# One residual, two engines: ScalarE scales four feature blocks of the mixer's reloaded residual, VectorE scales the other four inside its sums

## The chip, the cores and the metric

The kernel runs on one core of one Trainium2 chip. A core has five engines that take their own instruction streams in order and meet through semaphores: TensorE (PE; its weight loads are listed apart as PEld), VectorE (DVE), ScalarE (ACT), GpSimd (POOL) and SyncE (SP, here only an issuer of DMAs). The metric is the device time of one execution in microseconds; the kernel before takes 1076.38 us (median of three runs, 1075.28 to 1077.02).

## The reference

One decoder layer over 16 meta tokens and 512 real tokens with 1024 features: a SwiGLU feed-forward, a token mixer with two attention branches, a second feed-forward. All in float32. The change lies in the mixer's gates:

```python
def token_mixer(h, ...):
    proj = h @ w_in                       # h is rms_norm(residual, mix_norm)
    qa, ka, va, fa, qb, kb, vb, ga, gb = jnp.split(proj, idx, axis=-1)
    ...
    o_fox = fox_attention(qa, ka, va, log_f)
    o_swa = swa_attention(qb, kb, vb, swa_sinks, rel_bias_table)
    y = jax.nn.sigmoid(ga) * (o_fox @ w_branch_fox) + jax.nn.sigmoid(gb) * (o_swa @ w_branch_swa)
    return y @ w_out
```

`ga` and `gb` are products of the normalised residual with 2 x 1024 columns of `w_in`.

## The kernel before

**Number format.** A float32 product is made of three faster products. Each operand is split into a high part (ACT's cast, L133) and the rest (DVE's subtraction, L140); PE then does high x high (L301), high x rest (L302) and rest x high (L304). So every weight piece passes through ACT and then DVE before PE can use it: `raw` becomes `wh` and `wl`.

**Seven products for eight.** Two column blocks of weights (128 columns each) and the 512 tokens in two halves form a 2x2 block product, done with seven block products instead of eight (method `seven`). On the weights' side the pieces are A (a plain block, from `raw`), B (the sum `tc`, made by DVE from `rawC` and `rawD` in L233 and L234), C (`rawC`) and D (`rawD`, split into `wD`). On the activations' side the residual's features X (tokens in halves 0 and 1, features in halves 0 and 1) give A11, A12, A22 as they are and four sums: S3 = A11 - A21, S1 = A21 - A22, S2 = S1 - A11, S4 = A12 + S2. These are each a 128x1024 tile (four feature blocks of 128, each 256 tokens wide), and each is split like a weight (a cast and a subtraction). PE's order in one `seven` is A11 and S3 (with piece A), the S4 of the `seven` before, S2 and A22 (piece B), A12 and S1 (piece C). Each of the seven is 12 matmuls. After A11, ACT copies the accumulator `b` to a second bank `a` (L529), and PE then goes on adding S2 into `b`.

**The stage around the change.** After the attention, PE runs the last plain gate column, then six sliding-window branch products into `pt` banks, each copied out by ACT (L1722), and then the gates by `seven`: six of them in the order of the table `GATES`. To form the sums, the residual h1 is fetched again from DRAM by two DMAs on ACT's queue into `xg`, eight feature blocks of 128x512: blocks 0 to 3 by the first, 4 to 7 by the second. In the kernel before, ACT multiplies each of the eight blocks by the norm's gain `gmT` (L1728). S3 doesn't need `xg` (it is made of the split parts that still stand). DVE forms S1, S2 and S4 from `xg` (L1732, one instruction of 128x1024 each), into the tiles `at` that lie in `spare`. S4's sum is traced after the first `seven`.

**What sets the order.** No order is written out for the engines: a scheduler takes the traced program with its dependences and sets each engine's instruction order ahead of time; `after(...)` only puts the instructions of its block behind a named instruction on the same engine. On the chip each engine then follows its list. The other instructions that matter below are the gates' own arithmetic on DVE (L1754 before, L1766 after the change: products with `rb1`, `zA`, `oA`, `sg`), the sigmoids on ACT (L1794, then L1806) and the splits `yH`, `yL` of the finished gates. At the very start DVE scales the first token tiles by their norms (L649, L659), with the power on POOL (L351) in between; `gT` holds all gains and is fetched by SP's fourth DMA (L322), `gmT` is a slice of it.

Of the kernel before, what the change touches and what calls it, by code (L numbers as in the profile page):

```python
# [11 lines left out]
F32 = mybir.dt.float32  # L12
F32R = mybir.dt.float32r
AF = mybir.ActivationFunctionType
ALU = mybir.AluOpType
# [4 lines left out]
P = 128  # L20
D = 1024
KD = D // P
# [54 lines left out]
def run(steps):  # L77
    for f in steps:
        f()
# [3 lines left out]
def kernel(  # L83
# [22 lines left out]
    V, A, G, PE, SP = nc.vector, nc.scalar, nc.gpsimd, nc.tensor, nc.sync  # L106

    cp = ctx.enter_context(tc.tile_pool(name="const", bufs=1))
# [15 lines left out]
    def psum(whole=False):  # L124
        if banks["turn"] is not None:
            whole = banks["turn"] = not banks["turn"]
        tag = "pt" if whole else "ps"
        return pp.tile([P, 512], F32, tag=tag, name=nm(tag))

    def hi(o, i, scale=None):  # L130

        if scale is None:
            return A.copy(o, i)  # L133
        return A.activation(o, i, AF.Identity, scale=scale)

    def lo(o, i, h, scale=None):

        h = h.bitcast(F32)
        if scale is None:
            return V.tensor_tensor(out=o, in0=i, in1=h, op=ALU.subtract)  # L140
        else:
            return V.scalar_tensor_tensor(out=o, in0=i, scalar=scale, in1=h, op0=ALU.mult, op1=ALU.subtract)  # L142
# [59 lines left out]
    shared = {}  # L202
# [81 lines left out]
    def piece(ahead=None, then=None):  # L284

        c = state["use"]
        state["use"] += 1
        if then is not None and c in split:
            then(split[c])
            then = None  # L290
        split_to(c + (ahead or state["ahead"]))
        load_to(c + 5)
        if then is not None:
            then(split[c])
        return split.pop(c)
# [52 lines left out]
    gmT, g2T = gT[:, 1], gT[:, 2]  # L348
# [109 lines left out]
    class Units:  # L458
# [8 lines left out]
        def product(self, ps, name, w, half, more=False, first=True, last=True, src=None):  # L467

            h, l = (src or self.X.x)[name]
            n = len(h) if src else 4  # L470
            for k in range(n):
                prod(
                    [(ps[:, : self.th], h[k] if src else h[:, k], l[k] if src else l[:, k])],
                    w[0][:, n * half + k],
                    w[1][:, n * half + k],
                    k == 0 and first and not more,
                    k == n - 1 and last,
                    more,
                )
# [38 lines left out]
        def seven(self, use, last=False, src=None):  # L518

            th = self.th
            product = lambda *args: self.product(*args, src=src)
            b, a = psum(), psum(True)

            def p1(w):
                product(b, "A11", w, 0)
                A.copy(a[:, :th], b[:, :th])  # L529


            w = piece(None, p1)
            c = psum()
            product(c, "S3", w, 1)
            use("P7", c[:, :th])
            self.flush()
            w = piece()
            product(b, "S2", w, 0, True)
            d = psum(True)
            A.activation(d[:, :th], b[:, :th], AF.Identity, scale=-1.0)  # L540
            use("U2", b[:, :th])
            product(c, "A22", w, 1, True)
            use("C21 - U2", c[:, :th])
            w = piece()

            def p2():
                product(a, "A12", w, 1, True)
                use("C11", a[:, :th])

            def p5():  # L550
                product(d, "S1", w, 0, True)
                use("C22 + P7", d[:, :th])

            run([p5, p2] if last else [p2, p5])
            wd = piece(1 if last else None)

            def p3():
                product(d, "S4", wd, 0, True)
                use("C12", d[:, :th])

            self.pending = p3
            if last:
                self.flush()
# [44 lines left out]
    def after(*ins):  # L608

        st = ExitStack()  # L610
        for i in ins:
            st.enter_context(tc.issue_after(getattr(i, "ins", i)))
        return st
# [920 lines left out]
    for i in every:  # L1534
# [3 lines left out]
            out=zf[:n, i], in0=ps[:, 256:264], scalar=r1[:n, i : i + 1], in1=fb[:n], op0=ALU.mult, op1=ALU.add  # L1538
# [122 lines left out]
    halves = (slice(0, HF), slice(HF, S))  # L1661
# [17 lines left out]
    xg = gp.tile([P, KD, S], F32, tag="yH", name="xg")  # L1679
# [5 lines left out]
    at = [spare[:, 2 * i : 2 * i + 2].rearrange("p a (b c) -> p (a b) c", c=HF) for i in (0, 1, 2, 0)]  # L1685

    def parts_of(i, name):
        hi(xS[name][:, 0], at[i])
        lo(xS[name][:, 1], at[i], xS[name][:, 0])
# [34 lines left out]
    sliding(0, 1)  # L1724

    with after(*shared["split"]):
        for k in range(KD):
            A.activation(xg[:, k], xg[:, k], AF.Identity, scale=gmT[:, k : k + 1])  # L1728

    xq = lambda tok, feat: xg[:, 4 * feat : 4 * feat + 4, halves[tok]]  # L1730
    def sum_of(i, a, b, op=ALU.subtract):
        V.tensor_tensor(out=at[i], in0=a, in1=b, op=op)  # L1732

    parts_of(0, "S3")
    sum_of(1, xq(1, 0), xq(1, 1))
    sum_of(2, at[1], xq(0, 0))
    parts_of(2, "S2")
    parts_of(1, "S1")
    def last_sum():
        sum_of(3, xq(0, 1), at[2], ALU.add)  # L1740
        parts_of(3, "S4")

    sliding(*range(2, 6))

# [4 lines left out]
    class Gates:  # L1749
        th = HF  # L1750
# [73 lines left out]
    for i, step in enumerate(GATES):  # L1824
        if step[0] == "sliding":
            run(branch_steps(1, step[1], (oW, oLs), last_y(step[1])))
            gg.flush()
            continue
        b, m = step
        gg.seven(gate(m, b), False, src)  # L1830
        if i == 0:
            last_sum()
# [190 lines left out]
```

## Time and profile before

| what | value |
|---|---|
| median of three runs | 1076.38 us (1075.28 to 1077.02) |
| profiled execution | 1075.56 us, of it span 1073.5 us |
| granted TensorE clock | 0.999 of full speed |
| busy: PE, PEld | 1063.2 us (99%), 1031.0 us |
| busy: DVE, ACT, POOL | 892.0 us (83%), 654.6 us (61%), 211.7 us (20%) |
| ACT's scaling of `xg` (L1728) | 8 instructions, median 717 ns, from 604.4 to 610.2 us |
| DVE's sums from `xg` (L1732) | 3 instructions of 1217 to 1224 ns |

How to read it: times in the trace count from the first instruction of the span. A row of the timeline gives start, busy time, engine, line, operation, the tiles written and read, their shape, the count of merged instructions, and in brackets how long the engine had been idle before it and what ended that. Neighbouring instructions overlap in their pipelines, so the distance from start to start, not the busy time, is what one costs its engine. For PE the starts of neighbouring matmuls are the thing to look at.

### The profile page before, as it was taken

To read this page: it belongs to the slowest core of one execution; us is meant where nothing else is said; L and a number is where in the kernel's file an instruction comes from. 1 tells how busy PE (TensorE), PEld (TensorE's weight loads), DVE (VectorE), ACT (ScalarE), POOL (GpSimd) and SP (SyncE) were. 2 spreads that over 40 slices of the span, in tenths; PEclk is the share of its full clock that TensorE was granted. 3 is DMA by queue.
4 is the path that set the end of the run, shared out by engine and by line. 5 is a ranking of instruction groups with operands and counts; after the bars stand their busy time and mean duration, and the time that the engine had idled before them with its cause. 6 is when DMAs were issued, how large, how long until landed. Compare 5 with 4: busy or idle time off the path is not lost.

```text
span 1073.5 us, 22262 instructions
## 1 busy us (share of the span) xinstructions
PE 1063.2 (99%) x8515; PEld 1031.0 (96%) x8515; DVE 892.0 (83%) x1725; ACT 654.6 (61%) x1235; POOL 211.7 (20%) x281
## 2 busy tenths in 40 slices
PE   9999999999999999999999999999999999999998
PEld 8999999999999999999878799999999999999998
DVE  7988878888889678789897799888989788877895
ACT  7667456656666455556667766555665466745664
POOL 3011111121124442232200110001122111221120
PEclk9999999999999999999999999999999999999999
DMA  8787777688776314212211874567689777887763
GB/s 279 203 217 164 187 193 198 151 216 219 175 182 178 123 61 126 75 60 73 89 60 42 241 183 125 184 207 195 170 198 194 179 190 170 187 192 196 158 125 101
DMA packets 112570, 173.57 MB, mean 162 GB/s; under 512 B 10880, under 2 KB 59264, under 8 KB 112208
## 3 DMA queue, kind: packets, MB, share of 16 engines
q1 hardware_dynamic: 74464, 122.72, 36.2%
q0 software_dynamic: 29040, 37.83, 22.6%
q10 hardware_dynamic: 8960, 11.60, 3.4%
q8 instruction: 66, 1.08, 0.4%
q14 instruction: 40, 0.33, 0.1%
HBM read 167.89 MB, written 6.32 MB: 162 GB/s over the span
## 4 chain that ended last, share of the span: by engine, by line
PE 47%; DVE 5%; ACT 2%; DMA 1%; issue 1%; POOL 0%; ACTq 0%; SPq 0%; DVEq 0%; POOLq 0%
PE ps L301 8%; PE ps L304 8%; PE ps L302 8%; PE pt L301 7%; PE pt L302 7%; PE pt L304 7%; DVE wl L140 1%; DMA raw<-in_wg_dram 1%; ACT t L1209 1%; ACT wh L133 1%; DVE pL L140 1%; PE ps L1473 0%; PE ps L1938 0%; DVE S L140 0%; PE pt L1473 0%
## 5 line engine op out<-in xcount | busy, mean ns | idle before, releaser
L301 PE MATMUL ps<-x,wh 128*128 128x256 f32 (+2 forms) x768 | 219.7, 286 | 0.1
L302 PE MATMUL ps<-x,wh 128*128 128x256 f32 (+2 forms) x768 | 218.9, 285 | 0.5 <-DVE x L142 0.4
L304 PE MATMUL ps<-x,wl 128*128 128x256 f32 (+2 forms) x768 | 218.9, 285 | 0.0
L140 DVE TENSOR_TENSOR wl<-raw,wh 128x1024 fp32r<-128x1024 f32 (+3 forms) x125 | 150.1, 1201 | 39.8 <-ACT wh L133 38.9
L133 ACT CAST wh<-raw 128x1024 fp32r<-128x1024 f32 (+3 forms) x125 | 128.4, 1029 | 87.7 <-PE ps L302 52.5
L301 PEld LDWEIGHTS ps<-x,wh 128*128 128x128 f32 x768 | 144.7, 189 | 1.7 <-ACT hT L686 0.3
L302 PEld LDWEIGHTS ps<-x,wh 128*128 128x128 f32 x768 | 144.5, 188 | 1.4 <-DVE x L142 0.9
L304 PEld LDWEIGHTS ps<-x,wl 128*128 128x128 f32 x768 | 144.6, 188 | 0.9
L301 PE MATMUL pt<-x,wh 128*128 128x256 f32 (+2 forms) x424 | 125.3, 296 | 0.5 <-ACT wh L133 0.5
L304 PE MATMUL pt<-x,wl 128*128 128x256 f32 (+2 forms) x424 | 124.6, 294 | 0.0
L302 PE MATMUL pt<-x,wh 128*128 128x256 f32 (+2 forms) x392 | 112.5, 287 | 0.0
L133 ACT CAST wh<-tc 128x1024 fp32r<-128x1024 f32 (+1 forms) x70 | 71.8, 1026 | 65.1 <-DVE tc L234 55.7
L140 DVE TENSOR_TENSOR wl<-tc,wh 128x1024 fp32r<-128x1024 f32 (+1 forms) x70 | 83.5, 1192 | 32.4 <-ACT wh L133 32.0
L301 PE MATMUL ps<-acts,wh 128*128 128x264 f32 (+1 forms) x352 | 100.5, 285 | 0.1
L304 PE MATMUL ps<-acts,wl 128*128 128x264 f32 (+1 forms) x352 | 99.8, 284 | 0.0
L302 PE MATMUL ps<-acts,wh 128*128 128x264 f32 (+1 forms) x352 | 99.6, 283 | 0.0
L140 DVE TENSOR_TENSOR wl<-rawC,wh 128x1024 fp32r<-128x1024 f32 (+1 forms) x70 | 84.1, 1201 | 5.9 <-ACT wh L133 5.5
L133 ACT CAST wh<-rawC 128x1024 fp32r<-128x1024 f32 (+1 forms) x70 | 71.6, 1023 | 22.7 <-PE pt L302 17.7
L301 PEld LDWEIGHTS pt<-x,wh 128*128 128x128 f32 x424 | 79.9, 189 | 2.8 <-ACT wh L133 0.7
L304 PEld LDWEIGHTS pt<-x,wl 128*128 128x128 f32 x424 | 79.7, 188 | 2.1
L302 PEld LDWEIGHTS pt<-x,wh 128*128 128x128 f32 x392 | 73.8, 188 | 0.6
L301 PEld LDWEIGHTS ps<-acts,wh 128*128 128x128 f32 x352 | 66.5, 189 | 0.7 <-DVE h2T L918 0.3
(445 smaller groups left out, 3238.8 us busy)
## 6 DMA issues: line engine op xcount, KB each, us to landing
rawC<-in_w1i_dram SPq DMA_DIRECT2D x20, 512.0 KB, 5.1
raw<-in_w1i_dram SPq DMA_DIRECT2D x40, 256.0 KB, 4.5
raw<-in_w2i_dram SPq DMA_DIRECT2D x40, 256.0 KB, 3.3
rawC<-in_w2i_dram SPq DMA_DIRECT2D x20, 512.0 KB, 4.3
raw<-in_wm_dram SPq DMA_DIRECT2D x18, 512.0 KB, 4.3
raw<-in_wout_dram SPq DMA_DIRECT2D x16, 512.0 KB, 4.3
rawD<-in_w1i_dram SPq DMA_DIRECT2D x20, 256.0 KB, 4.3
raw<-in_w1i_dram POOLq DMA_DIRECT2D x20, 256.0 KB, 4.9
```

What stands on the lines that cost most here:

```text
L133: return A.copy(o, i)
L140: return V.tensor_tensor(out=o, in0=i, in1=h, op=ALU.subtract)
L301: PE.matmul(ps, sH, mH, start=first, stop=False, **more)
L302: PE.matmul(ps, sH, mL, start=False, stop=False, **more)
L304: shared["mm"] = PE.matmul(ps, sL, mH, start=False, stop=last, **more)
L1209: shared["exp"] = A.activation(t, t, AF.Exp, bias=nmx, scale=-1.0, accum_out=l[:, j : j + 1])
```

## The change

ACT now scales only blocks 0 to 3. A new small tile `less` holds minus the gains of blocks 4 to 7. DVE forms S1 and S4 with four SCALAR_TENSOR_TENSOR instructions each (block times gain, plus the other operand), one per feature block of 128x256; S2 stays one TENSOR_TENSOR. S4's two splitting instructions are put behind the first `seven`'s copy of `b` (L529).

```diff
             def p1(w):
                 product(b, "A11", w, 0)
-                A.copy(a[:, :th], b[:, :th])
+                shared["copy"] = A.copy(a[:, :th], b[:, :th])
...
     with after(*shared["split"]):
-        for k in range(KD):
+        for k in range(4):
             A.activation(xg[:, k], xg[:, k], AF.Identity, scale=gmT[:, k : k + 1])
+    less = cp.tile([P, 4], F32, name="less")
+    V.tensor_scalar(less, gmT[:, 4:KD], -1.0, None, op0=ALU.mult)
 
     xq = lambda tok, feat: xg[:, 4 * feat : 4 * feat + 4, halves[tok]]
-    def sum_of(i, a, b, op=ALU.subtract):
-        V.tensor_tensor(out=at[i], in0=a, in1=b, op=op)
+
+    def add_scaled(i, tok, by, to):
+        for k in range(4):
+            V.scalar_tensor_tensor(
+                out=at[i][:, k],
+                in0=xg[:, 4 + k, halves[tok]],
+                scalar=by[:, k : k + 1],
+                in1=to[:, k],
+                op0=ALU.mult,
+                op1=ALU.add,
+            )
 
     parts_of(0, "S3")
-    sum_of(1, xq(1, 0), xq(1, 1))
-    sum_of(2, at[1], xq(0, 0))
+    add_scaled(1, 1, less, xq(1, 0))
+    V.tensor_tensor(out=at[2], in0=at[1], in1=xq(0, 0), op=ALU.subtract)
     parts_of(2, "S2")
     parts_of(1, "S1")
     def last_sum():
-        sum_of(3, xq(0, 1), at[2], ALU.add)
-        parts_of(3, "S4")
+        add_scaled(3, 0, gmT[:, 4:KD], at[2])
+        with after(shared["copy"]):
+            parts_of(3, "S4")
```

The scheduler's lists differ in three places that matter. In the rows below a tile's name is followed by running numbers; `spare` holds the sums.

DVE at the head of the gates, before (`zA` is the last plain gate's product, L1709):

```order
L1709 TENSOR_TENSOR zA_4879<-zA_4879,spare_8183 128x512
L1732 TENSOR_TENSOR spare_8183<-xg_8197 128x1024
L140 TENSOR_TENSOR S3_1355_8196<-spare_8183,S3_1355_8196 128x1024
L1732 TENSOR_TENSOR spare_8183<-spare_8183,xg_8197 128x1024
L140 TENSOR_TENSOR S1_1347_8184<-spare_8183,S1_1347_8184 128x1024
L140 TENSOR_TENSOR wl_1369_8305<-raw_1360_8211,wh_1368_8304 128x1024
L140 TENSOR_TENSOR S2_1356_8198<-spare_8183,S2_1356_8198 128x1024
L233 TENSOR_TENSOR tc_1372_8336<-rawC_1364_8255,rawD_1365_8256 128x512
L140 TENSOR_TENSOR wD_1384_8411<-rawD_1365_8256,wD_1384_8411 128x512
L234 TENSOR_TENSOR tc_1372_8336<-tc_1372_8336,rawC_1364_8255 128x512
L1732 TENSOR_TENSOR spare_8183<-xg_8197,spare_8183 128x1024
L140 TENSOR_TENSOR wl_1374_8340<-tc_1372_8336,wh_1373_8339 128x1024
```

The same place after the change:

```order
L1736 SCALAR_TENSOR_TENSOR spare_8183<-xg_8197,less_8292 128x256
L1709 TENSOR_TENSOR zA_4879<-zA_4879,spare_8183 128x512
L1736 SCALAR_TENSOR_TENSOR spare_8183<-xg_8197,less_8292 128x256 x3
L1747 TENSOR_TENSOR spare_8183<-spare_8183,xg_8197 128x1024
L140 TENSOR_TENSOR S3_1355_8196<-spare_8183,S3_1355_8196 128x1024
L140 TENSOR_TENSOR S1_1347_8184<-spare_8183,S1_1347_8184 128x1024
L140 TENSOR_TENSOR S2_1356_8198<-spare_8183,S2_1356_8198 128x1024
L140 TENSOR_TENSOR wl_1369_8306<-raw_1360_8211,wh_1368_8305 128x1024
L233 TENSOR_TENSOR tc_1372_8337<-rawC_1364_8255,rawD_1365_8256 128x512
L140 TENSOR_TENSOR wD_1384_8412<-rawD_1365_8256,wD_1384_8412 128x512
L234 TENSOR_TENSOR tc_1372_8337<-tc_1372_8337,rawC_1364_8255 128x512
L1736 SCALAR_TENSOR_TENSOR spare_8183<-xg_8197,gT_82,spare_8183 128x256 x4
```

One of S1's four instructions now stands ahead of L1709, the rest right behind it; the splits of S3, S1, S2 and of the first weight piece follow in a block, then the sum `tc` of the first `seven`. Behind S4's four instructions come the splits of `tc` and `rawC`, and then S4's, which before stood behind six more rows. At the very start of DVE's list, the row `less` (L1730) has been placed between the first L649 and the first L659.

PE where S2 of the first `seven` begins, before and then after (`ps_1377` is bank b, `pt_1378` bank a, `wh_1373` and `wl_1374` are piece B, `wh_1379` is piece C):

```order
L304 MATMUL ps_1382_8396<-S3_1355_8196,wl_1369_8305 128x256
L301 MATMUL ps_1377_8373<-S2_1356_8198,wh_1373_8339 128x256
L302 MATMUL ps_1377_8373<-S2_1356_8198,wh_1373_8339 128x256
L301 MATMUL pt_1378_8374<-x_620_4306,wh_1379_8388 128x256
L304 MATMUL ps_1377_8373<-S2_1356_8198,wl_1374_8340 128x256
```

```order
L304 MATMUL ps_1382_8397<-S3_1355_8196,wl_1369_8306 128x256
L301 MATMUL ps_1377_8374<-S2_1356_8198,wh_1373_8340 128x256
L302 MATMUL ps_1377_8374<-S2_1356_8198,wh_1373_8340 128x256
L304 MATMUL ps_1377_8374<-S2_1356_8198,wl_1374_8341 128x256
L301 MATMUL ps_1377_8374<-S2_1356_8198,wh_1373_8340 128x256
```

The first matmul with piece C, which stood third in S2's run before, now stands behind S2's and A22's 24 matmuls.

ACT in the sixth and last `seven`, before and then after (`wh_1493` is its piece B, `wh_1497` its piece C, L529 its copy of b):

```order
L133 CAST yH_8371<-oA_4878 128x256 x2
L133 CAST wh_1493_9086<-tc_1492_9083 128x1024
L1794 ACTIVATE sg_1485_9036<-u2_1484_9032 128x256
L1794 ACTIVATE sg_1489_9058<-gz_1488_9056 128x256
L133 CAST wh_1497_9105<-rawC_1481_9001 128x1024
L529 COPY pt_1496_9091<-ps_1495_9090 128x256
```

```order
L133 CAST yH_8372<-oA_4878 128x256 x2
L1806 ACTIVATE sg_1485_9040<-u2_1484_9036 128x256
L1806 ACTIVATE sg_1489_9062<-gz_1488_9060 128x256
L133 CAST yH_8372<-oA_4878 128x256
L529 COPY pt_1496_9095<-ps_1495_9094 128x256
L1806 ACTIVATE sg_1491_9083<-c22_1490_9080 128x256
L133 CAST yH_8372<-oA_4878 128x256
L133 CAST wh_1493_9090<-tc_1492_9087 128x1024
L133 CAST wh_1497_9109<-rawC_1481_9005 128x1024
```

The casts of pieces B and C of the last `seven` now stand behind the copy of its bank b. DVE's list moved with it (`tc`'s second half L234 stands twelve rows behind the row that reads `u2` from its bank, where it stood one row behind it; most of what has come between is gate arithmetic), and on PE two matmuls with `wh_1497` and two of A22 stand ahead of the first matmul with piece B's rest.

## Prediction

> **What bounds the kernel now.** I read the page first (who is busy), then the windows around the change (who is idle there), then PE's timeline in the one window that isn't full, and last the timelines of the engines that feed it.
>
> ```profile
> PE 1063.2 (99%) x8515; PEld 1031.0 (96%) x8515; DVE 892.0 (83%) x1725; ACT 654.6 (61%) x1235; POOL 211.7 (20%) x281
> ```
>
> PE is the bound, so an edit on ACT and DVE is worth only what it changes in PE's gaps. By stretches (busy us of PE, PEld, DVE, ACT, POOL; clock; DMA share; GB/s):
>
> ```profile
> 604.00:611.00 7.00, 7.00 (x32) 5.67 (x31) 1.78 (x3) 6.61 (x12) 1.73 (x2) 1.00 1.06 344
> 611.00:618.00 7.00, 7.00 (x32) 5.66 (x31) 7.00 (x7) 5.64 (x8) 1.72 (x2) 1.00 0.76 140
> 618.00:628.00 10.00, 9.40 (x77) 8.99 (x76) 9.92 (x14) 7.39 (x13) 0.86 (x1) 1.00 0.68 195
> 628.00:638.00 10.00, 10.00 (x87) 10.00 (x86) 9.51 (x17) 6.27 (x13) 2.45 (x3) 1.00 0.74 189
> ```
>
> PE is full except from 618 to 628, where 0.60 us is missing. DVE idles 5.22 us from 604 to 611 and is nearly full from then on. DVE's late start is what the change can reach, and that one gap is where it can pay. PE's rows at the gap, where S2 of the first seven begins:
>
> ```profile
> 620.52 0.28 PE L302 MATMUL ps<-S,wh 128*128 128x256 f32 x1
> 620.64 0.28 PE L304 MATMUL ps<-S,wl 128*128 128x256 f32 x1
> 621.04 0.38 PE L301 MATMUL ps<-S,wh 128*128 128x256 f32 x1
> 621.27 0.28 PE L302 MATMUL ps<-S,wh 128*128 128x256 f32 x1
> 622.02 0.39 PE L301 MATMUL pt<-x,wh 128*128 128x256 f32 x1 [0.47 <-ACT wh L133]
> 622.25 0.28 PE L304 MATMUL ps<-S,wl 128*128 128x256 f32 x1
> ```
>
> Undisturbed starts lie 0.12 us apart (620.52 to 620.64; 0.118 over longer runs). From 620.64 to 622.25 are four steps, 0.47 us; they take 1.61. So **1.14 us** is lost, partly before the first row (bank b's copy) and mostly before the piece C matmul, which waits for ACT's cast of `rawC`.
>
> Why these are late, first ACT, then DVE:
>
> ```profile
> 606.62 1.34 ACT L1728 ACTIVATE xg<-xg,gT 128x512 f32<-128x512 f32 x2
> ...
> 608.33 2.57 ACT L1728 ACTIVATE xg<-xg,gT 128x512 f32<-128x512 f32 x4
> ...
> 618.18 0.59 ACT L1722 COPY oA<-pt 128x512 f32<-128x512 f32 x1 [1.54 <-PE pt L304]
> 619.67 1.06 ACT L133 CAST wh<-tc 128x1024 fp32r<-128x1024 f32 x1 [0.89 <-DVE tc L234]
> 620.63 0.36 ACT L529 COPY pt<-ps 128x256 f32<-128x256 f32 x1
> 620.93 1.04 ACT L133 CAST wh<-rawC 128x1024 fp32r<-128x1024 f32 x1
> ```
>
> ```profile
> 606.28 0.69 DVE L1709 TENSOR_TENSOR zA<-zA,spare 128x512 f32<-128x512 f32 x1 [1.27 <-ACT spare L1708]
> 610.93 1.22 DVE L1732 TENSOR_TENSOR spare<-xg 128x1024 f32<-128x1024 f32 x1 [3.95 <-ACT xg L1728]
> 612.07 1.22 DVE L140 TENSOR_TENSOR S<-spare,S 128x1024 fp32r<-128x1024 f32 x1
> ...
> 617.75 0.68 DVE L233 TENSOR_TENSOR tc<-rawC,rawD 128x512 f32<-128x512 f32 x1
> 618.35 0.68 DVE L140 TENSOR_TENSOR wD<-rawD,wD 128x512 fp32r<-128x512 f32 x1
> 618.95 0.68 DVE L234 TENSOR_TENSOR tc<-tc,rawC 128x512 f32<-128x512 f32 x1
> 619.55 1.22 DVE L1732 TENSOR_TENSOR spare<-xg,spare 128x1024 f32<-128x1024 f32 x1
> 620.76 1.23 DVE L140 TENSOR_TENSOR wl<-tc,wh 128x1024 fp32r<-128x1024 f32 x1
> ```
>
> The last four scalings hold ACT from 608.33 to 610.9. DVE waits for them (3.95 us), starts at 610.93, and reaches `tc` with L234 only at 618.95; ACT waits for that, and the copy of b and the cast of `rawC` queue behind its cast of `tc`.
>
> **The change part by part.**
>
> *Removed: four scalings on ACT*, 2.57 us to the end of the last, 0.62 us each. ACT isn't the bound there.
>
> *DVE's start.* It then waits for the second half of `xg` itself:
>
> ```profile
> L1732 DVEq EVENT_SEMAPHORE  x2: 21/36/50, 607.6 to 607.7; - x2
> DMA to landing us min/median/max: 8.4/9.8/11.2
> ```
>
> DVE's queue saw its waits end at 607.6 to 607.7 (the first row is of L1732, the second of `xg`'s two DMAs). The slower landing, 11.2 us, fits the second DMA. So the sums start at 607.7 instead of 610.93, 3.2 us earlier, with ACT's first four blocks ready (606.62 + 1.34, just before 608.0; the first of S1's four needs only the first of them). L1709 waits behind the first of the four and moves from 606.28 to about 608.1; its product is read only by the second branch's gates, which come behind the first two sevens.
>
> *Added: eight SCALAR_TENSOR_TENSOR for two TENSOR_TENSOR.* The trace has the same form (three SBUF float32 operands, 128x256, a gain per partition), and a two-operand row of that size beside it:
>
> ```profile
> 736.69 1.67 DVE L1863 SCALAR_TENSOR_TENSOR x<-h2T,gT,rb 128x256 f32<-128x256 f32 x4
> 682.25 1.42 DVE L140 TENSOR_TENSOR yL<-oA,yH 128x256 fp32r<-128x256 f32 x4
> ```
>
> With a last instruction of 0.48 and 0.41 us, steps are p = 0.40 and 0.34 us. A group of four is 1.6 us against 1.14 (610.93 to 612.07) for one wide instruction: 0.9 us more on DVE for both groups. The Trainium skill's Vector Engine (DVE) Microarchitecture Reference, section 7, Points that are easy to get wrong, says that this form with two SBUF sources that aren't bf16 halves the throughput. The two rows don't bear that out (a factor 1.18); what it would do is the third rival.
>
> *DVE's new timetable.* Up to `wl<-tc` it does S1's group (4p), L1709 (0.60, the step of the 128x512 rows), the sum for S2 and four splits (5 x 1.14 = 5.70), L233, `wD`, L234 (3 x 0.60), S4's group (4p), and the split of `tc` (1.23): 607.7 + 9.33 + 8p = 617.0 + 8p, **620.2** at p = 0.40. L234 starts at 607.7 + 1.6 + 0.6 + 5.7 + 1.2 = 616.8, before 618.95. ACT's cast of `tc` starts 0.72 after that, as now: 617.5 to 618.5; `rawC`'s follows to 619.5; the last `oA` copy to 620.0; L529 to 620.4. PE wants bank b at 620.76 (0.12 after 620.64) and `wl<-tc` at 621.0. Margins: 0.4 and 0.8 us. The piece C matmul now comes 24 matmuls later, at 623.6. So the gap closes: **-1.14 us**. Its bounds: -0.60, if only what the window shows as idle comes back, and -1.14, because PE's neighbouring stretches are full and can't give more. I take -1.14, since starts are what PE's pace shows.
>
> *S4's split behind L529*: ACT casts it at about 620.4, DVE subtracts it by 622.5; PE uses S4 after the second seven's S3, six products of 12 x 0.118 behind 620.76, at 629.2. Nothing waits.
>
> *`less`*: one small instruction in DVE's list at the start, where it waits for `gT`:
>
> ```profile
> 2.11 0.43 SPq L322 DMA_DIRECT2D gT<-in_gains_dram  x1
> DMA to landing us min/median/max: 4.9/4.9/4.9
> 6.91 0.75 DVE L659 TENSOR_SCALAR xt<-xt,rin 128x1024 f32<-128x1024 f32 x1 [0.83 <-POOL rin L351]
> 8.07 0.15 DVE L649 TENSOR_SCALAR rin<-rin 128x1 f32<-128x1 f32 x1 [0.41 <-ACT sq L634]
> ```
>
> `gT` lands at 2.1 + 4.9 = 7.0, DVE would have gone on at 6.91; with 0.15 for the instruction L659 slips about 0.25 us. Behind it DVE idles 0.41 before the next L649, which hides it: 0. If `gT` came later than about 7.2, the excess would lie on the path; bounds 0 and +0.3.
>
> *The last seven.* DVE and ACT run there in PE's rhythm, so I shift these rows by -1.14 and re-add them in the new order:
>
> ```profile
> 665.81 0.41 DVE L1754 TENSOR_TENSOR u<-ps,u 128x256 f32<-128x256 f32 x1
> 666.14 0.68 DVE L234 TENSOR_TENSOR tc<-tc,rawC 128x512 f32<-128x512 f32 x1
> 666.91 1.05 ACT L133 CAST wh<-tc 128x1024 fp32r<-128x1024 f32 x1 [0.58 <-DVE tc L234]
> 671.60 0.28 PE L301 MATMUL ps<-S,wh 128*128 128x256 f32 x1
> ```
>
> The `u` row now stands ahead of L233 and of one `oA` product: 665.81 - 1.14 - 0.60 - 0.34 = 663.73. Up to L234 follow L233 (0.60) and eleven steps of 0.335, `u` among them: 668.0. ACT's cast of `tc` 0.77 later, 668.8, ends 669.8; that of `rawC` (0.95 behind) ends 670.8. DVE's split of `tc` comes after L234 and four products, 668.0 + 0.60 + 1.34 = 670.0, and ends 671.2. PE starts S2 at 671.60 - 1.14 = 670.46 and wants `rawC`'s cast at the third matmul, 670.70, and `wl<-tc` at the seventh, 671.17. Both are level with their supply: **+0.2**, bounds 0 (DVE runs ahead) and +1.2 (one more DVE split or ACT round trip late).
>
> *Sum*: -1.14 + 0 + 0.2 = -0.9 us. The profiled execution, 1075.56, would be 1074.6; the median of the runs is 0.8 above it, so **1075.4 us**.
>
> **The rivals.**
>
> *The head start doesn't come.* DVE now depends on the second `xg` landing alone. The DMA share is 1.06 from 604 to 611, the busiest stretch here; 0.8 us later (608.5) uses up the margin, 2 us later gives the old gap back. Against: 607.7 was seen. Time: 1076.4.
>
> *The last seven takes it back* (the slower side). PE's list is fixed, and its third S2 matmul there stands behind two ACT casts, which stand behind twelve DVE rows with sigmoid round trips between them. Each us late is a us on PE. Above 1.14 the kernel is slower; a chain 2 us late gives 1076.4 - 1.14 + 2 = 1077.3. For: no margin, by the sum above. Against: most of what was put ahead is ready when DVE comes to it.
>
> *The dear form.* If a step of four is double the plain 0.335, p = 0.67, the split of `tc` ends at 622.4, 1.4 late at PE: 0.3 worse than the gap now, with the last seven 1076.9. It decides from p = 0.50 (level) and 0.64 (gain gone).
>
> **How the numbers follow.** Forecast (gap closed, up to 0.5 lost): 62 in 100. No head start: 13. Last seven: 15, about a third of it by more than 2 us net. Dear form: 3. Something unseen, either way: 7. A measurement here tells about 0.2% (2.15 us) from no change. The largest gain that PE's gap allows is half of that, so faster needs something unseen: 0.07. Slower needs a net 2.15: 0.08. Same: 0.85. The range takes the forecast with the runs' scatter (their median lies 0.6 and 1.1 from their ends) and the first two rivals: 1074.2 to 1077.2.
>
> **What would show it.** In the profile after: four L1736 rows on DVE from about 607.7, 1.6 us long; ACT's cast of `tc` at about 617.5; PE's starts 0.12 apart through S2 of the first seven, and PE full from 618 to 628; L659 at about 7.2 with the first L649 behind it unmoved; in the last seven, PE's third S2 matmul with a wait of 0.2 or less. The prediction is wrong if the gap stays, if a new one opens from 668 to 672, or if PE's starts stretch anywhere else by a microsecond.

## The result and the profile after

| | kernel before | change |
|---|---|---|
| median | 1076.01 us (1074.75 to 1078.31, 22 runs) | 1074.68 us (1073.81 to 1075.95, 22 runs) |
| span of the profiled execution | 1073.5 us | 1071.9 us |
| busy PE, DVE, ACT | 1063.2, 892.0, 654.6 us | 1062.0, 893.3, 652.8 us |

The ratio of the times is 0.9987, with a 95% interval of 0.9981 to 0.9993: 1.3 us less, between 0.75 and 2.0. The size is close to the sum that the prediction worked out (-0.9 us). Where it comes from is another matter: the runs below put about 0.7 us of it behind the gates, and some 0.15 us ahead of them, on something the prediction doesn't contain, and leave the rest of the gain, in the mixer's gates, at a size that depends on when a DMA lands.

First what the profile after shows of the predicted steps. The windows around the change (busy us of PE, PEld, DVE, ACT, POOL; clock; DMA share; GB/s):

```profile
604.00:611.00 7.00, 7.00 (x32) 5.68 (x31) 5.11 (x8) 6.35 (x10) 1.99 (x3) 1.00 1.01 323
618.00:628.00 10.00, 10.00 (x86) 9.92 (x85) 9.51 (x15) 7.25 (x13) 1.72 (x2) 1.00 0.74 197
```

DVE works 5.11 us from 604 to 611 where it worked 1.78, and the 0.60 us that PE lacked from 618 to 628 are there. DVE's timeline, from the second landing of `xg` on, and the landings of `xg`'s two DMAs:

```profile
606.60 0.49 DVE L1736 SCALAR_TENSOR_TENSOR spare<-xg,less 128x256 f32<-128x256 f32 x1 [1.85 <-DMA xg<-h1d]
607.01 0.69 DVE L1709 TENSOR_TENSOR zA<-zA,spare 128x512 f32<-128x512 f32 x1
607.61 1.27 DVE L1736 SCALAR_TENSOR_TENSOR spare<-xg,less 128x256 f32<-128x256 f32 x3
...
616.41 1.67 DVE L1736 SCALAR_TENSOR_TENSOR spare<-xg,gT,spare 128x256 f32<-128x256 f32 x4
617.99 1.22 DVE L140 TENSOR_TENSOR wl<-tc,wh 128x1024 fp32r<-128x1024 f32 x1
```

```profile
DMA to landing us min/median/max: 7.6/8.9/10.3
```

A group of four takes 1.58 us from start to start (616.41 to 617.99): the forecast's 1.6. The landing came after 10.3 us and not 11.2, so DVE began at 606.60 and not at 607.7; from there its list ran as worked out (split of `tc` finished 12.6 us later, 12.5 forecast). ACT and PE at the start of S2:

```profile
619.35 0.36 ACT L529 COPY pt<-ps 128x256 f32<-128x256 f32 x1
619.62 1.05 ACT L133 CAST S<-spare 128x1024 fp32r<-128x1024 f32 x1
620.60 1.05 ACT L133 CAST wh<-raw 128x1024 fp32r<-128x1024 f32 x1
621.55 0.37 ACT L1817 COPY p<-ps 128x256 f32<-128x256 f32 x1
```

```profile
620.52 0.28 PE L301 MATMUL ps<-S,wh 128*128 128x256 f32 x1
620.64 0.27 PE L302 MATMUL ps<-S,wh 128*128 128x256 f32 x1
...
621.82 0.28 PE L304 MATMUL ps<-S,wl 128*128 128x256 f32 x1
621.97 0.39 PE L301 MATMUL ps<-x,wh 128*128 128x256 f32 x1
622.20 0.28 PE L302 MATMUL ps<-x,wh 128*128 128x256 f32 x1
```

The copy of b is done long before PE wants the bank, and S2 runs in steps of 0.12. But A22's first matmul has steps of 0.15 and 0.23 about it, 0.14 us lost: its bank is emptied by the copy L1817, which now stands behind two casts, S4's among them. That wait is new.

The prologue, and the last seven (PE, then ACT):

```profile
7.04 0.17 DVE L1730 TENSOR_SCALAR less<-gT 128x4 f32<-128x4 f32 x1 [0.86 <-DMA gT<-in_gains_dram]
7.12 0.75 DVE L659 TENSOR_SCALAR xt<-xt,rin 128x1024 f32<-128x1024 f32 x1
8.09 0.15 DVE L649 TENSOR_SCALAR rin<-rin 128x1 f32<-128x1 f32 x1 [0.23 <-ACT sq L634]
```

```profile
670.46 0.28 PE L301 MATMUL ps<-S,wh 128*128 128x256 f32 x1
670.59 0.28 PE L302 MATMUL ps<-S,wh 128*128 128x256 f32 x1
670.83 0.39 PE L301 MATMUL pt<-x,wh 128*128 128x256 f32 x1
...
671.43 0.28 PE L304 MATMUL ps<-S,wl 128*128 128x256 f32 x1
```

```profile
669.73 1.05 ACT L133 CAST wh<-rawC 128x1024 fp32r<-128x1024 f32 x1
```

`less` holds L659 back by 0.21 and the next L649 by 0.02: hidden. In the last seven S2 begins at 670.46 as forecast, the third matmul waits for the cast of `rawC` that ends at 670.8, and the first product with piece B's rest starts at 671.43, 0.26 behind an undisturbed 671.17; 0.23 of this is lost about the third matmul.

Now the whole timetable of PE, before against after. PE's first 128x256 matmul of the gates starts at 617.93 before and 617.69 after; the first matmul of the last seven's last product at 675.86 and 674.96. So the gates are 57.93 and 57.27 us long: **0.66 us** gained, of 0.94 forecast. Beside the losses at A22 (0.14) and in the last seven (0.26), some 0.2 us are lost at 659 us, where PE passes to a product with `wD` (under 0.1 before); no row names the cause. 0.24 had come earlier (two executions of the kernel before differ by 0.36 there, from PE's first matmuls on; experiment 8 comes back to the 0.24). That makes 0.90 at 675 us; yet near the end of the span the lead is 1.57. The remaining 0.7 us arise in the second feed-forward, whose instructions the change doesn't touch. Two landmarks there, the second L368 row behind the gates (it spreads the second normalisation's factors for one half of the tokens) and the first transposition of the output, before and then after (the line numbers of the latter differ with the source):

```profile
735.59 0.61 PE L368 MATMUL ps<-ident,r 128*128 128x128 f32 x4
1046.12 1.18 PE L1938 MATMUL ps<-ident,h2T 128*128 128x128 f32 x8
```

```profile
734.73 0.61 PE L368 MATMUL ps<-ident,r 128*128 128x128 f32 x4
1044.56 1.20 PE L1950 MATMUL ps<-ident,h2T 128*128 128x128 f32 x8
```

310.53 us before, **309.83 us** after, with PE busy throughout in both, no wait that differs by more than 0.1 us, and a granted clock of 1.00 over the stretch in every execution shown here. Call this the second stretch; it gets experiments of its own.

### The profile page after: what moved, and what is told of

The parts are those of the page before. It is cut to its first block, busy times and chain, and to the rows that moved or that the text cites. A ratio compares the mean times of both kernels' runs of the same rounds, so it can differ in the third digit from the quotient of the medians.

```text
span 1071.9 us, 22258 instructions
## 1 busy us (share of the span) xinstructions
PE 1062.0 (99%) x8515; PEld 1029.7 (96%) x8515; DVE 893.3 (83%) x1732; ACT 652.8 (61%) x1231; POOL 211.8 (20%) x281
## 4 chain that ended last, share of the span: by engine, by line
PE 50%; DVE 3%; ACT 2%; issue 0%; DMA 0%; POOL 0%; ACTq 0%; DVEq 0%; POOLq 0%
PE ps L301 8%; PE ps L304 8%; PE ps L302 8%; PE pt L301 7%; PE pt L302 7%; PE pt L304 7%; ACT t L1209 1%; DVE wl L140 1%; ACT wh L133 1%; DVE pL L140 1%; PE ps L1473 0%; PE ps L1950 0%; PE pt L1473 0%; DMA raw<-in_wbr_dram 0%; DVE t L1212 0%
```

## The experiments

In all, PE's *gates* are the stretch from the first 128x256 matmul of the first seven to the last product of the last seven (57.93 us before), and the *second stretch* lies between the two landmarks above (310.53 us before).

**1. Both kernels once more.** The unchanged kernels, to see what differs from execution to execution.

> The changed kernel once more, unaltered. In its first profile PE's rows ran 0.24 us ahead of the kernel before when the gates began (617.69 against 617.93), 1.22 us ahead at the first S1 product, 0.90 us ahead behind the last seven, and then drew ahead steadily to 1.55 us at 1026, where no instruction differs. Theory (the late part is chance of one execution): this profile has the same gains and losses between 617 and 676 (gap closed, +0.15 us at A22 of the first seven, +0.23 us at S2 of the last seven), but not the same 0.6 us between 764 and 1026. Rival (the change also speeds up the second feed-forward): the 0.6 us come back. Time about 1.0 to 1.4 us under the kernel before.

> The kernel before once more, for a second profile. Theory: the gap of 1.1 us in S2 of the first seven is there again in the same rows, whether xg lands at 606.5 or 607.6 (ACT's last four scalings end near 610.9 in both); the pace of PE between 764 and 1026 differs from the first profile by tenths of a us, as a matter of the execution.

Measured: the change 1074.98 us, ratio 0.9994 (0.9985 to 1.0003), an interval that this time takes in no change; gates 57.60, second stretch 309.85. The kernel before 1075.39 us in one run; gates **57.31**, second stretch 310.54. So, against what was expected, the kernel before has not always the 1.14 us gap: here only 0.5 us were lost, all of it at the piece C matmul; the copy of b came in time, with `xg` landed 10.4 us after its issue and not 11.2.

```profile
621.76 0.38 PE L301 MATMUL pt<-x,wh 128*128 128x256 f32 x1 [0.25 <-ACT wh L133]
```

And the change has not always 57.27: here A22's first matmul waits longer for the copy behind S4's cast:

```profile
622.23 0.39 PE L301 MATMUL ps<-x,wh 128*128 128x256 f32 x1 [0.19 <-ACT p L1817]
```

The second stretch, by contrast, repeats to 0.02 us in both kernels: the theory that the late gain is chance of one execution falls, and its rival holds so far.

**2. The scaling alone, without S4's place.**

```diff
-        with after(shared["copy"]):
-            parts_of(3, "S4")
+        parts_of(3, "S4")
```

> The change without its second half: the scaling is shared out as in the change, S4's splits are not held behind the copy of b. ACT then casts S4 before rawC, and copies b after both. Theory (the head start of DVE pays, S4's place guards the copy of b): DVE's timetable as in the change, but the copy of b ends about 0.3 to 0.5 us after PE wants the bank (620.5), so S2 of the first seven starts that much late: 0.6 to 0.8 us under the kernel before. Rival (S4's place is what closes the gap): the old gap of 1.1 us stays.

Measured: 1075.82 us, ratio 1.0003 (0.9994 to 1.0012); gates 58.22. ACT, and PE at the start of S2:

```profile
618.66 1.05 ACT L133 CAST S<-spare 128x1024 fp32r<-128x1024 f32 x1 [0.53 <-DVE spare L1736]
619.61 0.58 ACT L1722 COPY oA<-pt 128x512 f32<-128x512 f32 x1
620.09 1.05 ACT L133 CAST wh<-rawC 128x1024 fp32r<-128x1024 f32 x1
621.04 0.37 ACT L529 COPY pt<-ps 128x256 f32<-128x256 f32 x1
```

```profile
621.47 0.39 PE L301 MATMUL ps<-S,wh 128*128 128x256 f32 x1 [0.83 <-ACT pt L529]
```

S4's cast waits for the sum in the middle of ACT's list, and the cast of `rawC` and the copy of b wait behind it. The head start of DVE is spent there: S2 starts 1.1 us late, where 0.3 to 0.5 was expected, so the rival (the old gap stays) has the size right, though all of it now lies at the copy of b. So the second part of the change is not an ornament: without it the gates are no shorter than before. (The other half alone, S4's parts behind the copy in the kernel before, gives the same instruction lists as the kernel before on every engine, and so is no kernel of its own.)

**3. The new order of PE alone.** In the kernel before, the first seven's A12 product is put behind A22's, as the change's schedule has it.

```diff
+            if "pin" in shared:
+                shared["pin"] = [shared["mm"]]
...
-                product(a, "A12", w, 1, True)
+                with after(*shared.pop("pin", ())):
+                    product(a, "A12", w, 1, True)
```

> The kernel before with one edit: in the first seven the products with piece C are put behind A22's on PE, as the scheduler puts them in the change; ACT still scales all eight blocks. Theory (the weights of piece B come late because DVE starts late): piece C's matmul no longer waits, but the third matmul of S2 now waits for piece B's rest, which DVE ends at 622.0; S2's loss shrinks from 1.14 us to about 1.0. Rival (the piece C matmul in third place was the cause, and its move alone is the gain): the gap falls to 0.3 us or less, and the time is that of the change.

Measured: 1075.84 us, ratio 1.0001 (0.9992 to 1.001); gates 58.08, second stretch 310.54. PE no longer waits for the cast of `rawC`, but for the copy of b and then for piece B's rest:

```profile
621.52 0.39 PE L301 MATMUL ps<-S,wh 128*128 128x256 f32 x1 [0.27 <-ACT pt L529]
622.52 0.39 PE L304 MATMUL ps<-S,wl 128*128 128x256 f32 x1 [0.49 <-DVE wl L140]
```

Together 1.3 us are lost (about 1.0 expected; `xg` landed late here, 11.7 us after its issue). The order alone moves the wait and doesn't shorten it; the supply must be earlier.

**4. Doses of delay.** One or three idle DVE instructions of 1.14 us each stand ahead of S1's group and take the head start away.

```diff
-    add_scaled(1, 1, less, xq(1, 0))
+    for _ in range(1):
+        idle = V.tensor_tensor(out=at[2], in0=xq(1, 1), in1=xq(1, 1), op=ALU.subtract)
+    with after(idle):
+        add_scaled(1, 1, less, xq(1, 0))
```

> The change with one idle 128x1024 TENSOR_TENSOR (1.14 us, from raw xg into a tile that the next sum overwrites) put in front of S1's group on DVE. Theory (what counts is when DVE reaches the split of tc): in the change's profile that split ended at 619.2 and PE wanted it at 620.75, 1.5 us of margin, with xg landed at 606.5. One step of delay leaves 0.4 us: no gap. The scheduler gives this kernel the last seven's order of the kernel before, so that wait is gone too: PE is 1.0 to 1.2 us ahead behind the last seven. If xg lands at 607.6 as in the kernel before, a gap of 0.7 us. Rival (any later start costs in proportion): 1.1 us lost.

> The same with three idle instructions, 3.4 us of delay. Theory: DVE's head start of 3.2 to 4.4 us is spent; the split of tc ends near 622.6 and the copy of b near 622.2, 1.8 to 2 us behind PE's wish: the old gap is back and somewhat longer, time 0 to 1.5 us above the kernel before. Rival (the gain doesn't hang on DVE's start): as fast as the change.

Measured: one dose 1075.59 us, ratio 0.9997 (0.9987 to 1.0006), gates 59.24; three doses 1076.9 us, ratio 1.0011 (1.0002 to 1.0021), gates 59.38. Delay does reach PE at the copy of b, as the theory has it, but the two doses cost nearly the same, not 1 to 3. PE with one dose:

```profile
622.28 0.39 PE L301 MATMUL ps<-S,wh 128*128 128x256 f32 x1 [1.15 <-ACT pt L529]
624.73 0.39 PE L301 MATMUL ps<-x,wh 128*128 128x256 f32 x1 [0.76 <-ACT p L1820]
```

Two things spoil the dose. `xg` landed 11.9 us after its issue with one dose and 10.6 with three, a difference of more than one dose by itself. And the scheduler orders the lists anew: with one dose it put the last instruction of S4's group behind two splits, so that S4's cast holds ACT until 624.4 and the copy that A22 needs follows it, at 624.31. With three doses PE loses 1.4 us at the copy of b, nothing at A22, 0.5 in later sevens and 0.8 in the last. The doses show the direction; they don't measure a slope.

**5. `less` out of the prologue.**

```diff
-    V.tensor_scalar(less, gmT[:, 4:KD], -1.0, None, op0=ALU.mult)
+    with after(shared["split"][1]):
+        V.tensor_scalar(less, gmT[:, 4:KD], -1.0, None, op0=ALU.mult)
```

> The change with the small instruction that negates the gains held back to the place where it is used, out of the prologue. Theory (it hides in a wait of DVE): L659 starts at 6.9 instead of 7.1, and PE's first feed-forward matmul at the same time as in the change, within 0.1 us. Rival (it costs its 0.2 us): PE starts 0.2 us earlier than in the change.

Measured, one run: 1077.29 us; gates 57.28, second stretch 309.89, both as in the change. The time is no evidence: the granted clock fell in the first 20 us (after the window's busy times: clock, DMA share, GB/s),

```profile
12.00:16.00 4.00, 3.63 (x17) 3.10 (x16) 3.71 (x8) 2.97 (x8) 2.09 (x3) 0.51 1.04 408
```

and to 0.63 from 16 to 20 us, and PE was 2.2 us behind by 30 us of the span. In the four traces of the two unchanged kernels the clock is 1.00 there. Before the clock fell, L659 started at 6.92, as expected, and PE's first feed-forward matmul at 11.01, not earlier than the change's 10.79; so the rival (0.2 us earlier) isn't seen, but the executions scatter from 10.4 to 11.1 there. That `less` is hidden rests on the row of L649 above.

**6. S4's parts further back.** Since A22's copy waits behind S4's cast, the parts go behind that copy too (behind the copy of `u2`).

```diff
-        with after(shared["copy"]):
+        with after(shared["u2"]):
             parts_of(3, "S4")
...
-                A.copy(u2, box["u2"])
+                shared["u2"] = A.copy(u2, box["u2"])
```

> The change with S4's two splitting instructions put behind the first seven's copy of U2 instead of its copy of b (two words in the source). In the scheduler's lists the copy of P7 then stands directly behind the next weight's cast, ahead of S4's cast, and the last seven keeps the order of the kernel before. Theory (two small new waits eat 0.4 us of the gain: A22 of the first seven waits 0.15 us for the copy of P7 behind S4's cast, S2 of the last seven 0.23 us for weights that the scheduler put late): both waits are gone, PE is 1.1 us ahead of the kernel before behind the last seven, 0.4 us more than the change; time about 0.4 us under the change, too little to be told by the times alone. Rival (these waits are only moved on, S4 being late for its own product): PE waits at the second seven's S4 product, near 629.

Measured: 1074.18 us, ratio 0.9988 (0.9979 to 0.9997); gates **57.23**, although `xg` landed as late as 11.8 us after its issue. PE lost 0.43 us at the copy of b and no more than 0.1 at any other place of the gates, neither at A22 nor in the last seven:

```profile
620.88 0.39 PE L301 MATMUL ps<-S,wh 128*128 128x256 f32 x1 [0.17 <-ACT pt L529]
```

In the same series the change took 1074.98 us (0.9994); the intervals overlap, so that this version is better than the change is told by the waits that are gone, not by the times.

**7. The second stretch: the tile alone.** Every kernel so far that contains the change had the second stretch at 309.8 to 309.9 us, and the two without it at 310.5. What could reach that far is the place of things in memory: `less` is a new tile of 16 bytes a partition in the pool of constants, and everything laid out behind it moves. So the tile and the instruction that fills it were put into the kernel before, read by nothing.

```diff
+    less = cp.tile([P, 4], F32, name="less")
+    V.tensor_scalar(less, gmT[:, 4:KD], -1.0, None, op0=ALU.mult)
```

> The kernel before with only the tile `less` (16 bytes a partition) and the one instruction that fills it; nothing reads it, and the gates run as before. In the traces so far every kernel that has this tile gained a further 0.7 us on the TensorE timetable, evenly between 690 and 1067 us of the span (after +0.72, scale_only +0.74, dose1 +0.71, dose3 +0.72), and the two without it did not (order_only +0.01, before_again -0.09), though the instructions there are the same. Theory 1 (place in memory: the tile moves what is laid out after it): TensorE between 690 and 1067 us is again 0.7 us (0.6 to 0.8) quicker than in the first profile of before, while the gates lose their 0.5 to 1.3 us as before does; the time lies 0.7 us under that of before, a ratio of 0.9993 to 0.9994. Theory 2 (the stretch gains because of the new order in the gates, such as an earlier start of the weights' transfers): 0.0 to 0.1 us between 690 and 1067 us, ratio 1.000.

And the other way round, the change with `less` in free columns of a tile that is there already:

```diff
-    A.activation(warm, nhalf, AF.Silu)
+    A.activation(warm[:, :4], nhalf[:, :4], AF.Silu)
...
-    less = cp.tile([P, 4], F32, name="less")
+    less = warm[:, 4:]
```

> The change with `less` kept in four free columns of a tile that is there already (warm), so that no tile is added and the instructions stay as in the change. Theory 1 (place in memory): the gates gain as in the change (0.3 to 0.7 us between 618 and 676 us of the span), and between 690 and 1067 us TensorE runs at the pace of before, 0.0 to 0.1 us ahead instead of 0.7; the time is 0.3 to 0.7 us under before, ratio 0.9994 to 0.9997. Theory 2 (the order in the gates): 0.7 us there as in the change, ratio 0.9987 to 0.999.

Measured: the tile alone 1074.51 us, ratio **0.9991** (0.9982 to 0.9999); the change without the tile 1076.27 us, ratio **1.0003** (0.9994 to 1.0012). The landmarks, the tile alone first, then the change without it:

```profile
735.28 0.61 PE L368 MATMUL ps<-ident,r 128*128 128x128 f32 x4
1045.15 1.20 PE L1941 MATMUL ps<-ident,h2T 128*128 128x128 f32 x8
```

```profile
736.45 0.61 PE L368 MATMUL ps<-ident,r 128*128 128x128 f32 x4
1046.96 1.19 PE L1950 MATMUL ps<-ident,h2T 128*128 128x128 f32 x8
```

309.87 and 310.51 us. The second stretch follows the tile, not the gates: the first theory holds, the second falls. And in the change without the tile, no gain in time can be told (0.3 to 0.7 us were expected).

That run had the latest landing relative to PE, and shows what the change does then:

```profile
608.75 0.48 DVE L1736 SCALAR_TENSOR_TENSOR spare<-xg,warm 128x256 f32<-128x256 f32 x1 [3.49 <-ACT xg L1728]
```

```profile
621.49 0.39 PE L301 MATMUL ps<-S,wh 128*128 128x256 f32 x1 [0.30 <-ACT pt L529]
623.68 0.38 PE L301 MATMUL ps<-x,wh 128*128 128x256 f32 x1 [0.50 <-ACT p L1817]
```

DVE began at 608.75 (the row names ACT, but its first block had been done for more than 2 us; the second landing, 11.9 us after an issue at 596.7, was at 608.6), and PE lost 0.57 and 0.77 us. The gates took 58.51 us, longer than in any execution of the kernel before, where the first theory had them shorter.

**8. How far the addresses move.** In the built program the 16 bytes are rounded up to 32. PE's large operands (the weights' parts `wh` and `wl`, the activations `acts2`, `x2`) start 96 bytes behind a multiple of 128 in the kernel before, and on one with the tile. Two more sizes of the unread tile, 64 bytes a partition as below and 96 (`[P, 24]`):

```diff
-    less = cp.tile([P, 4], F32, name="less")
+    less = cp.tile([P, 16], F32, name="less")[:, :4]
```

> As pad_only, with the unread tile 64 instead of 16 bytes a partition. In the built program each address behind the tile stands 64 bytes further than in before (pad_only and the change: 32, to which the 16 are rounded up). The large tiles (wh, wl, x, acts2, zA) start at 32 bytes behind a multiple of 64 in before, on a multiple of 64 (of 128 too) in pad_only, and here at 32 behind a multiple of 64 again. Theory 1 (alignment): nothing is gained between 690 and 1067 us of the span (0.0 to 0.1 us on the TensorE timetable against the first profile of before), ratio 1.000. Theory 2 (any shift away from the old addresses, or the tile and its instruction as such): 0.6 to 0.7 us there as in pad_only, ratio 0.9991 to 0.9994.

> As pad_only, with the unread tile 96 bytes a partition: every address behind it stands 96 bytes further than in before, so that the large tiles start on a multiple of 64 that is not one of 128. Theory 1 (alignment to 64): 0.6 to 0.7 us gained between 690 and 1067 us of the span, ratio 0.9991 to 0.9994. Theory 1b (alignment to 128): 0.0 to 0.3 us there, ratio 0.9997 to 1.000. Theory 2 (any shift): as pad_only, 0.6 to 0.7 us, so that pad64 and not this run tells theory 2 from theory 1.

Measured: with 64 bytes 1074.85 us, ratio 0.9996 (0.9987 to 1.0005); with 96 bytes 1075.12 us, ratio 0.9998 (0.9989 to 1.0006). These times can't tell the two apart. The landmarks can, 64 bytes first and then 96:

```profile
734.88 0.61 PE L368 MATMUL ps<-ident,r 128*128 128x128 f32 x4
1044.65 1.19 PE L1941 MATMUL ps<-ident,h2T 128*128 128x128 f32 x8
```

```profile
735.03 0.60 PE L368 MATMUL ps<-ident,r 128*128 128x128 f32 x4
1045.54 1.18 PE L1941 MATMUL ps<-ident,h2T 128*128 128x128 f32 x8
```

| start of the operands, bytes behind a multiple of 128 | kernels | second stretch, us |
|---|---|---|
| 0 (shift 32) | the change, again, experiments 2, 4, 5, 6, and the tile alone (8 executions) | 309.81 to 309.89 |
| 32 (shift 64) | tile of 64 bytes | 309.77 |
| 64 (shift 96) | tile of 96 bytes | 310.51 |
| 96 (no shift) | the kernel before, again, experiment 3, the change without the tile (4 executions) | 310.51 to 310.54 |

Alignment to 64 or to 128, theories 1 and 1b, falls: the shift of 64 gains although it leaves the start off both, and the shift of 96 doesn't although it reaches a multiple of 64. "Any shift" falls with the shift of 96. Where in the stretch the time goes, the traces tell. These windows count only the matmuls that read `wD`, the split of piece D, between 736 and 1046 us (PE busy us, matmuls; clock; DMA share; GB/s): the kernel before, the tile alone, 64 bytes, 96 bytes.

```profile
736.00:1046.00 310.00, 46.06 (x345) 1.00 0.78 179
736.00:1046.00 310.00, 45.28 (x345) 1.00 0.78 180
736.00:1046.00 310.00, 45.34 (x345) 1.00 0.78 180
736.00:1046.00 310.00, 45.80 (x345) 1.00 0.77 180
```

With the tile alone and with 64 bytes these matmuls take 0.78 and 0.72 us less, about as much as the whole stretch gains (0.66 and 0.76), though they are one in seven of its matmuls. With 96 bytes they take 0.26 less, and the other matmuls take as much more; so its 310.51 is a sum of two opposite differences and not the pace of before, and the two levels of the table are no rule. In the built programs this `wD` lies at the same address in all four, and the activations that it is multiplied with move. So it isn't the weights' own shift that speeds these products up. Whether the activations' address by itself counts or its distance from `wD`, and whether anything goes modulo 128, was not tried and is open.

The stretch ahead of the gates shows the shift too. From 30 to 320 us (the first feed-forward) PE's starts gain 0.15 to 0.19 us on the first execution of the kernel before in the eight executions with a shift of 32, and 0.07 with 64; they lose 0.16 with 96 and stay within 0.03 without a shift. Of the 0.24 us that the change was ahead when its gates began, 0.16 came there.

## Why the prediction was right, and where it was not

First the gates of ten executions in one table (those of experiments 2, 3 and 4 stand there), worked out from the timelines; times are counted from PE's first matmul of the gates, and "first scaling" is ACT's first block of `xg`, which starts when the first DMA has landed.

| kernel | first scaling | copy of b (L529) | gates, us |
|---|---|---|---|
| kernel before | -13.54 | +2.70 | 57.93 |
| kernel before, again | -14.44 | +2.08 | 57.31 |
| tile alone (gates as before) | -13.57 | +2.67 | 57.90 |
| tile of 64 bytes (gates as before) | -14.17 | +2.07 | 57.30 |
| tile of 96 bytes (gates as before) | -15.17 | +2.06 | 57.26 |
| change | -14.32 | +1.66 | 57.27 |
| change, again | -13.57 | +1.99 | 57.60 |
| change, `less` late | -13.86 | +1.66 | 57.28 |
| change, without the tile | -13.12 | +2.86 | 58.51 |
| S4's parts further back | -13.39 | +2.72 | 57.23 |

**DVE's head start: mechanism right, its base a matter of luck.** DVE starts at the second landing, as forecast. From its start to the copy of b it is 12.3 us in the change (607.32 to 619.62 again, 608.75 to 621.06 without the tile; 12.75 in the first profile) and 9.7 in the kernel before (610.93 to 620.63). In the three executions of the change with the copy at +1.99 or earlier PE doesn't wait for it, as forecast. But the landing scatters: 10.3 to 11.9 us for the second DMA in the change's versions, where the prediction took one value and gave a landing 0.8 us later a chance of 13 in 100. Whether the change itself shifts the landing can't be told: 9.7 to 11.7 us in the six executions in which ACT scales all blocks. That rival (no head start) came about in part in one of the four executions of the change, the one without the tile: a start 1.05 us later than forecast, the copy late by 0.57 at PE.

**The gap of before, -1.14: the term that was mis-sized.** It was read from one execution. Among the five with the gates of before, two took 57.9 us for the gates and three 57.3: with an early landing the copy of b comes in time there too, and only some 0.5 us is lost. A still earlier landing brings nothing more: ACT's last four scalings stand behind a copy L1722 that waits for PE (it waits 0.17 us in the kernel before, again, and 0.73 with the tile of 96 bytes). Against the late kind (first scaling about 13.55 ahead) the change gained 0.3 (57.60 against 57.93 and 57.90); against the early kind nothing (57.27 and 57.28 against 57.26 to 57.31). Averaged over these executions the change's gates take 57.67 us and those of before 57.54. So at least half of the gain of 0.66 us between the two first profiles was the landing, and with the addresses of before the change's ratio is 1.0003 (0.9994 to 1.0012).

**The SCALAR_TENSOR_TENSOR steps: right.** A step of 0.40 us was forecast, and 1.58 us for a group of four measured. The rival of the dear form (0.67) is out. The Trainium skill (Vector Engine (DVE) Microarchitecture Reference, section 7, Points that are easy to get wrong) says that this form with two SBUF sources that aren't bf16 halves the throughput; measured against the two-operand form, this trace doesn't agree for this size (0.40 against 0.335).

**S4's split, "nothing waits": wrong.** The step looked at who reads S4 and not at what stands behind its cast on ACT: the copy L1817, for which PE waits before A22. 0.14 us in the first profile, 0.46 in the second, 0.77 without the tile. Experiment 6 moves the parts behind that copy, and the wait is gone. Experiment 2 shows that this edit can't be dropped either.

**`less`: right.** L659 moved by 0.21 us (0.25 forecast), L649 by 0.02. What the tile does by being there was not on the list: the prediction priced its instruction and not its 32 bytes.

**The last seven, +0.2: right.** 0.26 us, nearly all at the first of the two places named, the cast of `rawC`. That S2's start came out to the hundredth (670.46) is luck: counted from the gates' first matmul it came 0.90 earlier than before and not 1.14, and the other 0.24 had come ahead of the gates. In experiment 6, whose lists differ there, it isn't lost. That the last seven takes more than the gain, the rival on the slower side, was not seen in any execution of the change.

**The sum.** Forecast -0.9; the medians differ by -1.3. Of that, 0.7 is the second stretch, shown by experiments 7 and 8 to come from the addresses, and some 0.16 the first feed-forward, which goes with them; the rest is within what the landings scatter. So that the number came out is luck: the gap's term was one execution's landing (against executions with a like landing the gates gained 0 to 0.3 us), A22's wait was put at nothing, and a term of 0.7 us is not in the sum. The prediction bounded the gain by PE's gap, since the neighbouring stretches are full; the second stretch got shorter with PE busy throughout. The likeliest case, a time within 0.2% of before, is what was measured. The prediction's own sign of failure, "if PE's starts stretch anywhere else", was worded one-sidedly: they shrank somewhere else.

## What to carry to other kernels

Before a gain of a microsecond is put down to an edit, compare the stretches that the edit doesn't touch: here half of it lay behind the change's stage, in identical instructions, and a tile that nothing reads brought it alone. A gap that hangs on a DMA's landing is to be read from several executions of the same kernel, since one profile shows only one draw. When a piece of work is moved back in an in-order list, look not only at who waits for its result but at who stands behind it on its engine.

## What the runs showed of the hardware

- PE's pace in a long run of 128x256 matmuls depends slightly on where tiles lie in SBUF: 309.8 or 310.5 us for the same instructions (0.2%), at full granted clock, repeatable to 0.08 us among the eight executions with a shift of 32 bytes and to 0.03 among the four without. Nearly all of the gain lies in the matmuls with `wD`, whose weights stay in place while their activations move: 46.06 us busy before, 45.28 and 45.34 with shifts of 32 and 64 bytes, 45.80 with 96. No row shows it as a wait.
- The landing of a fetch of 1 MB (four blocks of 128x512 float32) on ACT's queue, in the same place of the same program, took 10.3 and 11.1 us for the second of the two in two executions of the change, and between 9.7 and 11.9 in the other versions, without any edit that touches it. With the gates of the kernel before, two executions with 11.2 us took 0.6 us longer for them than three with 9.7 to 10.6.
- A SCALAR_TENSOR_TENSOR of 128x256 float32 with three operands in SBUF costs 0.40 us from start to start, against 0.335 for a TENSOR_TENSOR: 1.2 times.
